# Hybrid encoder trunk on one core: the opening stage without low parts on GpSimd, and its weight pieces stored by GpSimd's queue

## The chip, the core and the metric

The program runs on one core of a Trainium2 chip. The core has a matrix engine (TensorE, PE in the rows, with its weight loads as PEld), VectorE (DVE), ScalarE (ACT), GpSimd (POOL) and SyncE (SP), which here only issues transfers. ScalarE and GpSimd issue transfers too. Each engine takes its instructions in the order in which they stand in its queue, and waits at an instruction until what it needs is there. Sixteen DMA engines move data between the memory of the chip (HBM) and the core's own memory (SBUF). The metric is the device time in microseconds of one execution; lower is better.

## The reference

Two independent batches of 512 rows by 1024 columns, `x_prompt` and `x_sample`, pass through the same layer. Only the opening of the layer matters here:

```python
c_act = jax.nn.silu(c)
mod = c_act @ w_ada[l] + b_ada[l]                      # 1024 -> 6 * 1024
sh1, sc1, g1, sh2, sc2, g2 = [m[:, None, :] for m in jnp.split(mod, N_MOD, axis=-1)]
h = rms_norm(x, norm1_g[l]) * (1.0 + sc1) + sh1
proj = h @ w_in[l]                                     # 1024 -> 2816
q_a, k_a, v_a, q_r, k_r, v_r, g_r = jnp.split(proj, IN_OFFSETS, axis=-1)
```

After it come windowed attention (on the first 768 columns of `proj`: 512 of q, 128 of k, 128 of v), bidirectional retention (the other columns), an output projection, a second modulated norm, and a squared-ReLU MLP. Weights and activations are 32-bit floats.

## The kernel before, in words

Every large product is made of three matmuls. An operand is split into a high part (a copy in the type fp32r) and a low part (the operand minus its high part); high times high, high times low and low times high are added up in a bank of PSUM. The function `mm3` (lines 128 to 130) issues the three. So every weight tile and every activation tile needs one copy (on ScalarE or VectorE) and one subtraction before the matrix engine can take it.

**The opening stage** (lines 974 to 1181) computes, for batch 0, eight column groups of 128 features, called `kc` = 0 to 7. For each group it needs the shift and scale of that group, which are sums over the whole of `w_ada` columns (`ada_sums`, matmuls of line 216 into `pm`, copied out as `mr` by ScalarE at line 221, transposed into `pmt` at line 229, added up into `mod_s` and `mod_a` by VectorE). Then `prepare` makes the modulated group `hm` from the transposed rows `xT`, and its high and low parts in `h` (lines 326 to 328). Then `products` multiplies `h` with six pieces of the matching 128 rows of `w_in` (the first 768 columns) into six open banks named `first`: 18 matmuls for a group. The rows of `x` are first normalised (`x_rstd`, `x_scale`) and transposed (`x_columns`, into banks `px`).

The weights of the stage come in three kinds. `raw_ada` of groups 0 and 1 ("ones"): four tiles of 512 KB, each by two transfers (line 985). `raw_ada` of group pairs 2, 4 and 6 ("pairs"): four tiles of 512 KB for a pair, two for the scale and two for the shift (line 89). `raw_wi`: eight tiles of 128 by 768, 384 KB each (line 89). High parts are `wh_ada` and `wih`, low parts `wl_ada` and `wil`. Before the change, the low part of every second `pairs` tile and of seven of the eight `raw_wi` tiles is computed by GpSimd, the others by VectorE; the high part of seven `raw_wi` tiles is a VectorE copy (line 1024).

The order of the work on each engine is the order in which the stage's code is written: `pin(start)` ties each instruction to the one before it on its engine, up to the products of group 5. Outside it a scheduler orders the instructions. Transfers of SP go out in order too. The tiles of the stage named by `r4` share 32 buffers, and the raw tiles of `w_in` from group 2 on share three (tag `raw`): a load waits until the last reader of the buffer's old content is done.

Batch 1 uses the same first 768 columns later (near 210 to 250 us). Its split pieces are not made again: `products` stores `wih` and `wil` of each group to HBM (line 1048, tensor `kept_first`), and `kept_unit` (line 119) loads them back, 12 loads of 512 KB: high and low parts for k, v and four pieces of q. Before the change `kept_first` is laid out so that each of the 12 loads reads 4 KB in one run per partition, and the stores, issued by ScalarE's queue, write runs of 512 bytes.

The small vectors `dec` (decays) and `sink` are loaded by GpSimd's queue, spread over 128 partitions, before the opening stage starts.

## Time and profile before

| what | value |
|---|---|
| median of 3 runs | 1155.02 us (1154.34 to 1156.5) |
| profiled execution, its own time | 1155.35 us |
| span of the profiled execution | 1153.5 us |
| TensorE busy | 1108.4 us, 96% of the span |
| VectorE busy | 899.6 us, 78% |
| ScalarE busy | 497.6 us, 43% |
| GpSimd busy | 68.2 us, 6% |

Times in rows are counted from the start of the span. In rows of the timeline the first number is the start, the second the duration, and the brackets at the end hold the idle time of that engine just before, with what ended it. In rows of groups, `x6: 1212/1221/3393` are count and shortest, median and longest duration in ns. A matmul's duration contains the pipeline's length: matmuls of 128x512 that follow each other start 0.23 us apart, whatever their duration says.

### The profile page before, as it was taken

Reading aid. Unit: us, or ns where it says so; the run is one execution under the profiler, and the core shown is the slowest. Engines: PE = TensorE matmul, PEld = TensorE weight load, DVE = VectorE, ACT = ScalarE, POOL = GpSimd, SP = SyncE. Lnnn points to the kernel's source line nnn. Section 1 sums busy time; section 2 is a strip of 40 time slices with the busy share of each in tenths; the row PEclk is TensorE's granted clock in tenths of the full one; section 3 lists DMA queues with packets and bytes.
Section 4 is the critical chain, followed back from the end, with each engine's and each line's share of the span. In section 5 each row is a group of like instructions: output and inputs, shape, how many; then the busy total and the mean of one; then the engine's idle time right before and its main releaser. Section 6 shows DMA issues by size and latency. Waiting matters only on the chain.

```text
span 1153.5 us, 14407 instructions
## 1 busy us (share of the span) xinstructions
PE 1108.4 (96%) x5167; PEld 903.5 (78%) x5167; DVE 899.6 (78%) x1496; ACT 497.6 (43%) x847; POOL 68.2 (6%) x79
## 2 busy tenths in 40 slices
PE   5989999999999999998999999999989999999995
PEld 3668787778888878887888888888778888888884
DVE  4888988978888687699998778876659655679675
ACT  4446765435554243355333333333434542335341
POOL 3620001100000000000000000000000000000011
PEclk9999999999999999999999999999999999999999
DMA  9786677665454689950655455442793455625503
GB/s 287 243 268 223 206 233 265 221 204 172 160 178 159 194 282 325 351 185 26 210 195 179 161 169 177 170 162 103 258 356 99 147 190 183 226 84 183 183 19 145
DMA packets 125135, 224.36 MB, mean 194 GB/s; under 512 B 8500, under 2 KB 59780, under 8 KB 125064
## 3 DMA queue, kind: packets, MB, share of 16 engines
q1 hardware_dynamic: 112168, 217.14, 55.9%
q10 hardware_dynamic: 12544, 6.29, 1.9%
q8 instruction: 40, 0.66, 0.2%
q0 software_dynamic: 352, 0.03, 0.2%
q14 instruction: 31, 0.25, 0.1%
HBM read 152.36 MB, written 71.06 MB: 194 GB/s over the span
## 4 chain that ended last, share of the span: by engine, by line
PE 78%; DVE 9%; DMA 7%; ACT 2%; issue 2%; POOL 1%; POOLq 0%; SPq 0%; ACTq 0%; DVEq 0%
PE x L1326 13%; PE px_None L937 12%; PE y L1326 11%; PE py_None L937 9%; PE po L129 2%; PE po L130 2%; PE po L128 2%; PE po L429 1%; PE ppt L422 1%; PE psc L396 1%; PE pj_rv L128 1%; PE pj_rv L130 1%; PE pj_rv L129 1%; PE pj_rg L130 1%; PE pj_rg L128 1%
## 5 line engine op out<-in xcount | busy, mean ns | idle before, releaser
L843 DVE TENSOR_TENSOR uc_l<-ur,uc_h 128x1024 fp32r<-128x1024 f32 x56 | 68.3, 1221 | 48.2 <-ACT uc_h L842 31.2
L1326 PE MATMUL x<-wc_h,uc_h 128*128 128x512 f32 x256 | 99.9, 391 | 4.4 <-DVE acc L1367 3.7
L1326 PE MATMUL x<-wc_l,uc_h 128*128 128x512 f32 x256 | 99.7, 390 | 0.0
L1326 PE MATMUL x<-wc_h,uc_l 128*128 128x512 f32 x256 | 99.7, 389 | 0.0
L842 ACT CAST uc_h<-ur 128x1024 fp32r<-128x1024 f32 x56 | 58.8, 1050 | 74.4 <-PE x L1326 22.7
L1326 PE MATMUL y<-wc_l,uc_h 128*128 128x512 f32 x192 | 75.6, 394 | 3.5 <-DVE wc_l L843 3.5
L1326 PE MATMUL y<-wc_h,uc_l 128*128 128x512 f32 x192 | 75.3, 392 | 0.0
L1326 PE MATMUL y<-wc_h,uc_h 128*128 128x512 f32 x192 | 75.2, 392 | 0.0
L842 ACT CAST wc_h<-w 128x1024 fp32r<-128x1024 f32 x48 | 50.4, 1050 | 49.9 <-PE x L1326 19.4
L843 DVE TENSOR_TENSOR wc_l<-w,wc_h 128x1024 fp32r<-128x1024 f32 x48 | 58.5, 1219 | 6.5 <-ACT wc_h L842 4.5
L1326 PEld LDWEIGHTS x<-wc_h,uc_h 128*128 128x128 f32 x256 | 48.1, 188 | 15.6 <-DVE acc L1367 4.5
L1326 PEld LDWEIGHTS x<-wc_h,uc_l 128*128 128x128 f32 x256 | 48.1, 188 | 10.0
L1326 PEld LDWEIGHTS x<-wc_l,uc_h 128*128 128x128 f32 x256 | 48.1, 188 | 9.9
L128 PE MATMUL po<-wh_wo,ms 128*128 128x512 f32 x128 | 50.5, 397 | 1.9 <-ACT ms L761 1.9
L129 PE MATMUL po<-wl_wo,ms 128*128 128x512 f32 x128 | 49.8, 391 | 0.3 <-DVE wl_wo L103 0.3
L130 PE MATMUL po<-wh_wo,ms 128*128 128x512 f32 x128 | 49.7, 391 | 0.0
L255 DVE SCALAR_TENSOR_TENSOR adacc_c<-raw_ada_c,cact,adacc_c 128x512 f32<-128x512 f32 x56 | 39.8, 746 | 8.6 <-DMA raw_ada_c<-in_w_ada_dram 7.6
L1326 PEld LDWEIGHTS y<-wc_l,uc_h 128*128 128x128 f32 x192 | 36.4, 190 | 11.6 <-DVE wc_l L843 4.0
L842 ACT CAST wc_s4h<-raw_w 128x1024 fp32r<-128x1024 f32 x16 | 16.9, 1054 | 62.6 <-PE px_None L937 41.6
L406 ACT ACTIVATE st<-st,negm 128x256 f32<-128x256 f32 (+1 forms) x64 | 35.2, 555 | 19.4 <-DVE negm L401 19.4
L1326 PEld LDWEIGHTS y<-wc_h,uc_l 128*128 128x128 f32 x192 | 36.5, 190 | 7.5
L1326 PEld LDWEIGHTS y<-wc_h,uc_h 128*128 128x128 f32 x192 | 36.4, 189 | 7.6
(380 smaller groups left out, 3083.3 us busy)
## 6 DMA issues: line engine op xcount, KB each, us to landing
ur<-spill SPq DMA_DIRECT2D x56, 512.0 KB, 4.1
raw_w<-in_w_mlp_dram SPq DMA_DIRECT2D x32, 512.0 KB, 3.9
spill<-s SPq DMA_DIRECT2D x64, 256.0 KB, 3.7
w<-in_w_mlp_dram SPq DMA_DIRECT2D x32, 512.0 KB, 7.0
spill<-u SPq DMA_DIRECT2D x48, 256.0 KB, 2.0
raw_ada_g<-in_w_ada_dram SPq DMA_DIRECT2D x16, 512.0 KB, 4.6
raw_ada_c<-in_w_ada_dram SPq DMA_DIRECT2D x16, 512.0 KB, 4.0
raw_ada<-in_w_ada_dram SPq DMA_DIRECT2D x12, 512.0 KB, 8.8
```

What stands on the lines that cost most here:

```text
L128: nc.tensor.matmul(ps, lhs[0], rhs[0], start=start, stop=False)
L129: nc.tensor.matmul(ps, lhs[0], rhs[1], start=False, stop=False)
L130: nc.tensor.matmul(ps, lhs[1], rhs[0], start=False, stop=stop)
L255: nc.vector.scalar_tensor_tensor(acc[b], src, cb, acc[b], ALU.mult, ALU.add)
L396: nc.tensor.matmul(psc[:, :w], qs[hh][:, isl], k_[:, s, j0 * P:j1 * P], start=(s == 0), stop=(s == 1))
L406: nc.scalar.activation(st[hh][:, :w], st[hh][:, :w], AF.Exp, bias=negm[:, hh:hh + 1], scale=0.125, accum_out=den[:, hh:hh + 1])
L422: nc.tensor.transpose(pt[:, hh * P:(hh + 1) * P], st[hh][:, jj * P:(jj + 1) * P], ident)
L429: nc.tensor.matmul(po, va[:, j0 + jj, g].rearrange("p s e -> p (s e)"), pts[jj][:, s, :], start=(jj == 0 and s == 0), stop=(jj == nj - 1 a ...
L842: nc.scalar.copy(hi, src)
L843: nc.vector.tensor_sub(lo, src, f(hi))
L937: self.last = nc.tensor.matmul(bank[:, cs], x[:, k, :], y, start=first and k == 0 and i == 0, stop=last and k == 3 and i == 2, skip_group_ ...
L1326: nc.tensor.matmul(out, left[n][x][:, i, ts_], right[n][y][:, i, :], start=first and i == 0 and k == 0, stop=end and i == 1 and k == 2, sk ...
```

## The change

What it does, in eight parts:

1. Every low part of the opening stage is computed by VectorE (`low_pair`, `low_one`, `split_wi`, `split_unit` lose their argument for the engine). Every high part `wih` is a copy on ScalarE.
2. The third and fourth row tiles of `x` no longer load one after the other: `x_2` as before, then the tiles of ones of group 0, then `x_3`, then `raw_wi` of group 0. The norm, scaling and transposing of each row tile are written out in the order of arrival, `x_3` after the sums of group 0. The conditioning vectors (`cond`) come after the transposes of `x_0` and `x_1` in the matrix engine's order.
3. The modulated group 0 is made by ScalarE alone: two activations with scale and bias, one straight into the high part, one into `hm`; VectorE only subtracts.
4. Loads of `dec` and `sink` move from before the stage to a place behind the second batch of low parts (`head_loads`); on GpSimd's queue they stand right behind the four small powers of the row norms.
5. The distance mask for the attention (`masked_distance`, three VectorE instructions on `di`) moves from the time of group 1 to just before group 2 is modulated; `sink8` moves further down.
6. `kept_first` is laid out by group of rows: the stores, now on GpSimd's queue, write runs of 3 KB, one transfer for a high or low part.
7. The 12 loads of batch 1 gather eight runs of 512 bytes for each partition.
8. The copy of `xT` of group 0 goes from ScalarE to VectorE.

```diff
-    def split_unit(src, name, lo_engine, pool=None):
+    def split_unit(src, name, pool=None):
         t = raw_unit(src, name)
         w = split_high(t, name, pool)
-        lo_engine.tensor_sub(w[1], t, f(w[0]))
+        nc.vector.tensor_sub(w[1], t, f(w[0]))
...
-            nc.sync.dma_start(f(t), kept[key][:, s, :])
             w.append(t.rearrange("p (a n) -> p a n", n=n))
+            src = kept[key][:, s]
+            nc.sync.dma_start(f(w[s]) if len(src.shape) == 3 else f(t), src)
...
+    def head_loads():
+        nc.gpsimd.dma_start(dec[:, 0, :], decay_f.broadcast_to([P, RH]))
+        nc.gpsimd.dma_start(dec[:, 1, :], decay_b.broadcast_to([P, RH]))
+        nc.gpsimd.dma_start(sink, attn_sink.broadcast_to([P, AH]))
...
+        if which == b == kc == 0:
+            for d in (dst[:, 0, :], t):
+                nc.scalar.activation(d, src, AF.Identity, bias=mod_s[0][:, kc, 0:1], scale=mod_a[0][:, kc, 0:1])
+            nc.vector.tensor_sub(dst[:, 1, :], t, f(dst[:, 0, :]))
+            return dst
...
-    xt0 += [load_x_tile(0, t) for t in range(2, NT)]
+    xt0.append(load_x_tile(0, 2))
...
-    def low_pair(kc, s, kh, engine):
+    def low_pair(kc, s, kh):
         t, w = pairs[kc, s, kh]
-        engine.tensor_sub(w[1], t, f(w[0]))
+        nc.vector.tensor_sub(w[1], t, f(w[0]))
...
-    def split_wi(kc, engine=nc.vector, low=nc.gpsimd):
+    def split_wi(kc):
         w = [r4(f"wi{s}_{kc}").rearrange("p a n -> p (a n)")[:, :768] for s in "hl"]
-        if engine is nc.scalar:
-            nc.scalar.copy(w[0], wi[kc][:, :768])
-        else:
-            nc.vector.tensor_copy(w[0], wi[kc][:, :768])
-        low.tensor_sub(w[1], wi[kc][:, :768], f(w[0]))
+        nc.scalar.copy(w[0], wi[kc][:, :768])
+        nc.vector.tensor_sub(w[1], wi[kc][:, :768], f(w[0]))
...
-                    nc.scalar.dma_start(kept_first[:, :, s, k * P:(k + 1) * P],
-                                        f(wi[k][s]).rearrange("p (c n) -> p c n", n=P))
+                    nc.gpsimd.dma_start(kept_first[:, k, s, :], f(wi[k][s]))
-    kept_first = tc.dram_tile((P, 6, 2, 1024), F32, name="kept_first")
+    kept_first = tc.dram_tile((P, KC, 2, 768), F32, name="kept_first")
     for c in range(6):
-        kept[f"in{c * P}"] = kept_first[:, c]
+        kept[f"in{c * P}"] = kept_first.rearrange("p k s n -> p s k n")[:, :, :, c * P:(c + 1) * P]
...
         ones.append(load_one(kc))
+        if kc == 0:
+            xt0.append(load_x_tile(0, 3))
         load_wi(kc)
...
-    tables = bias_tables(masked_distance())
     split_wi(1)
     high_pair(2, 1)
-    low_pair(2, 1, 0, nc.vector)
-    low_pair(2, 1, 1, nc.gpsimd)
+    low_pair(2, 1, 0)
...
     prepare(1)
+    low_pair(2, 1, 1)
     high_pair(2, 0)
-    low_pair(2, 0, 0, nc.vector)
-    low_pair(2, 0, 1, nc.gpsimd)
+    low_pair(2, 0, 0)
+    low_pair(2, 0, 1)
+    head_loads()
...
     next(g)
+    tables = bias_tables(masked_distance())
     next(tables)
     prepare(2)
```

Line numbers of the changed kernel are some 3 to 8 higher than before; names in the rows below are those of the code with a running number behind them.

The first place is GpSimd's queue in the opening stage, from the last two powers of the row norms on. Before:

```order
L306 TENSOR_TENSOR rr_x_2_198<-rv_x_2_196,neghalf 128x1
L306 TENSOR_TENSOR rr_x_3_208<-rv_x_3_206,neghalf 128x1
L1025 TENSOR_TENSOR wil_241<-raw_wi_130,wih_240 128x768
L1025 TENSOR_TENSOR wil_287<-raw_wi_138,wih_286 128x768
L1002 TENSOR_TENSOR wl_ada_2_1_1_294<-raw_ada_2_1_1_142,wh_ada_2_1_1_293 128x1024
L1002 TENSOR_TENSOR wl_ada_2_0_1_341<-raw_ada_2_0_1_146,wh_ada_2_0_1_340 128x1024
L1025 TENSOR_TENSOR wil_358<-raw_wi_148,wih_357 128x768
```

and with the change:

```order
L309 TENSOR_TENSOR rr_x_2_198<-rv_x_2_196,neghalf 128x1
L309 TENSOR_TENSOR rr_x_3_229<-rv_x_3_227,neghalf 128x1
L159 DMA dec<-in_ret_decay_fwd_dram 128x4
L160 DMA dec<-in_ret_decay_bwd_dram 128x4
L161 DMA sink<-in_attn_sink_dram 128x8
L1053 DMA kept_first<-wih_248 128x768
L1053 DMA kept_first<-wil_249 128x768
L1053 DMA kept_first<-wih_278 128x768
L1053 DMA kept_first<-wil_279 128x768
```

Thirteen subtractions are gone, and nothing but transfers is left; a store stands behind nothing but the stores before it, so it goes out as soon as its piece is split, where before it stood in ScalarE's queue behind the products of the next group.

The second place is VectorE's queue between the modulated groups 1 (`hm_0_1`) and 2 (`hm_0_2`). Before:

```order
L326 TENSOR_SCALAR hm_0_1_333<-xT_245,mod_a_103,mod_s_105 128x512
L328 TENSOR_TENSOR h_0_1_332<-hm_0_1_333,h_0_1_332 128x512
L1002 TENSOR_TENSOR wl_ada_2_0_0_338<-raw_ada_2_0_0_144,wh_ada_2_0_0_337 128x1024
L1024 CAST wih_357<-raw_wi_148 128x768
L232 COPY m_2_1_398<-pmt_1_395 128x8
L234 TENSOR_TENSOR ms_1_400<-m_2_1_398 128x4
L202 TENSOR_SCALAR mod_a_103<-ms_1_400,onep,cols 128x2 x2
L232 COPY m_2_0_435<-pmt_0_432 128x8
```

and with the change:

```order
L334 TENSOR_SCALAR hm_0_1_324<-xT_252,mod_a_100,mod_s_102 128x512
L336 TENSOR_TENSOR h_0_1_323<-hm_0_1_324,h_0_1_323 128x512
L1010 TENSOR_TENSOR wl_ada_2_1_1_286<-raw_ada_2_1_1_139,wh_ada_2_1_1_285 128x1024
L1010 TENSOR_TENSOR wl_ada_2_0_0_330<-raw_ada_2_0_0_141,wh_ada_2_0_0_329 128x1024
L1010 TENSOR_TENSOR wl_ada_2_0_1_333<-raw_ada_2_0_1_143,wh_ada_2_0_1_332 128x1024
L1030 TENSOR_TENSOR wil_353<-raw_wi_145,wih_352 128x768
L235 COPY m_2_1_393<-pmt_1_390 128x8
L237 TENSOR_TENSOR ms_1_395<-m_2_1_393 128x4
```

Three subtractions of tiles of `w_ada` and one of `w_in` stand where one subtraction and one copy stood; the three instructions on `di` follow later, between `mod_s` of this pair and `hm_0_2`.

The third place is SP's queue where batch 1 loads the kept pieces (`wh` high, `wl` low). Before:

```order
L119 DMA wl_k_2375<-kept_first 128x1024
L119 DMA wh_k_2373<-kept_first 128x1024
L119 DMA wh_v_2377<-kept_first 128x1024
L119 DMA wl_v_2379<-kept_first 128x1024
L563 DMA kept_t_115<-dtab_2_2284 128x896
```

and with the change:

```order
L121 DMA wl_k_2375<-kept_first 128x8x128
L121 DMA wh_k_2373<-kept_first 128x8x128
L121 DMA wh_v_2377<-kept_first 128x8x128
L121 DMA wl_v_2379<-kept_first 128x8x128
L121 DMA wh_q_0_2457<-kept_first 128x8x128
```

Each load is in the same place but made of eight short runs for each partition; `kept_t`, a store, has moved two loads down.

## The prediction

> **What bounds the kernel now.** I read the page first, then the opening stage by stretches of 10 us, then VectorE and GpSimd side by side in the timeline, the matrix engine's idle brackets, and the transfers of the first 90 us.

> ```profile
> span 1153.5 us, 14407 instructions
> PE 78%; DVE 9%; DMA 7%; ACT 2%; issue 2%; POOL 1%; POOLq 0%; SPq 0%; ACTq 0%; DVEq 0%
> 30.00:40.00 10.00, 7.87 (x46) 5.14 (x45) 9.24 (x8) 4.99 (x7) 7.95 (x5) 0.87 0.53 175
> 40.00:50.00 10.00, 9.66 (x51) 6.89 (x49) 8.11 (x12) 4.39 (x8) 4.07 (x3) 0.96 0.98 315
> 60.00:70.00 10.00, 7.82 (x51) 5.14 (x49) 8.36 (x17) 4.27 (x8) 4.40 (x3) 1.00 0.86 243
> ```

> The chain that ends last is 78% matrix engine, so time can only be won where that engine idles. The change touches the opening stage, and there it does. The rows of stretches give the busy time of PE, PEld, DVE, ACT and POOL, the granted clock, and the DMA share with GB/s: between 30 and 40 us the matrix engine works 7.87 us, VectorE is busy 9.24 us with only eight instructions, and the clock falls to 0.87. Why eight instructions fill 9 us, the timeline shows:

> ```profile
> 27.39 1.22 DVE L1002 TENSOR_TENSOR wl_ada<-raw_ada,wh_ada 128x1024 fp32r<-128x1024 f32 x1
> 29.45 1.16 DVE L326 TENSOR_SCALAR hm<-xT,mod_a,mod_s 128x512 f32<-128x512 f32 x1
> 33.34 3.39 DVE L1002 TENSOR_TENSOR wl_ada<-raw_ada,wh_ada 128x1024 fp32r<-128x1024 f32 x1
> 37.51 4.01 DVE L202 TENSOR_SCALAR mod_a<-ms,onep,cols 128x2 f32<-128x2 f32 x2
> ...
> 70.52 1.29 DVE L234 TENSOR_TENSOR ms<-m 128x4 f32<-128x4 f32 x1
> ...
> 33.24 2.41 POOL L1002 TENSOR_TENSOR wl_ada<-raw_ada,wh_ada 128x1024 fp32r<-128x1024 f32 x1 [0.37 <-ACT wh_ada L97]
> 37.33 1.83 POOL L1025 TENSOR_TENSOR wil<-raw_wi,wih 128x768 fp32r<-128x768 f32 x1 [1.68 <-issue]
> 39.12 2.37 POOL L1002 TENSOR_TENSOR wl_ada<-raw_ada,wh_ada 128x1024 fp32r<-128x1024 f32 x1
> ```

> The same subtraction takes VectorE 1.22 us alone and 3.39 us when GpSimd works from 33.24 to 35.65; two tiny instructions that start at 37.51 end at 41.5, when GpSimd's second piece ends. From 29.45 to 70.52 eleven instructions are stretched so; against their ordinary lengths the excess is 16.9 us. [...]

> What reaches the matrix engine is less than 16.9 us. These are the places that I use as checkpoints (the second matmul of a group waits for the low part of `h`):

> ```profile
> 24.94 0.50 PE L129 MATMUL first<-h,wih 128*128 128x512 f32 x1 [0.22 <-DVE h L328]
> 36.79 0.28 PE L216 MATMUL pm<-wl_ada,c 128*4 128x256 f32 x1 [1.77 <-DVE wl_ada L1002]
> 40.87 0.28 PE L229 MATMUL pmt<-ident,mr 4*128 4x4 f32 x2
> 44.17 0.39 PE L129 MATMUL first<-h,wih 128*128 128x512 f32 x1
> 58.62 0.50 PE L129 MATMUL first<-h,wih 128*128 128x512 f32 x1 [0.85 <-DVE h L328]
> 66.08 0.28 PE L229 MATMUL pmt<-ident,mr 4*128 4x4 f32 x2 [2.10 <-ACT mr L221]
> 74.09 0.50 PE L129 MATMUL first<-h,wih 128*128 128x512 f32 x1
> 82.54 0.39 PE L130 MATMUL first<-h,wil 128*128 128x512 f32 x1
> ```

> Groups 0, 2, 4 and 6 start (by their second matmul) at 24.94, 44.17, 58.62 and 74.09, and the last product starts at 82.54. Behind that the matrix engine is nearly full, so I let a gain at the end of the stage go through to the end of the program.

> **The change part by part.** Durations for the moved pieces, from the groups of the two raw tiles:

> ```profile
> L1025 POOL TENSOR_TENSOR wil<-raw_wi,wih x7: 1827/1854/2767, 18.2 to 69.9; 128x768 fp32r<-128x768 f32 x7
> L1024 DVE CAST wih<-raw_wi x7: 547/552/554, 26.9 to 74.2; 128x768 fp32r<-128x768 f32 x7
> L1022 ACT CAST wih<-raw_wi x1: 832/832/832, 17.3 to 17.3; 128x768 fp32r<-128x768 f32 x1
> L1025 DVE TENSOR_TENSOR wil<-raw_wi,wih x1: 959/959/959, 74.8 to 74.8; 128x768 fp32r<-128x768 f32 x1
> L97 ACT CAST wh_ada<-raw_ada x14: 1038/1044/1053, 14.6 to 64.7; 128x1024 fp32r<-128x1024 f32 x14
> L1002 POOL TENSOR_TENSOR wl_ada<-raw_ada,wh_ada x6: 2371/2482/2587, 30.3 to 65.8; 128x1024 fp32r<-128x1024 f32 x6
> ```

> VectorE gains six subtractions of 1.22 and seven of 0.96 us, 14.0 us; it loses seven copies of 0.55 (3.9 us) and the 16.9 us of stretching: 6.8 us less over the stage. ScalarE gains seven copies of 0.83, 5.8 us, and loses the issuing of 16 stores. But the subtractions now stand in one queue where two engines worked side by side, so the totals settle nothing; I walk the chain between checkpoints.

> *To group 0.* Before, the square sum of `x_2` waits for its transfer:

> ```profile
> 11.69 1.06 ACT L317 ACTIVATE jk<-x 128x1024 bf16<-128x1024 f32 x1 [1.54 <-DMA x<-in_x_prompt_dram]
> 15.09 2.82 PE L1068 MATMUL px<-ident,x 128*128 128x128 f32 x12 [2.27 <-DVE x L321]
> GB/s 38 351 94 232 365 277 287 313 340 350 347 374 370 348 357 185 4 22 330 317 352 307 289 267 126 157 0 177 167 351 346 344 162 380 357 371 231 369 401 362
> q0 software_dynamic: 96, 0.01, 2.1%
> raw_ada<-in_w_ada_dram SPq DMA_DIRECT2D x12, 512.0 KB, 8.8
> raw_wi<-in_w_in_dram SPq DMA_DIRECT2D x8, 384.0 KB, 5.8
> kept_first<-wih ACTq DMA_DIRECT2D x8, 384.0 KB, 4.6
> ```

> The GB/s row has 40 slices of 2.25 us. In the third and fourth (4.5 to 9 us) the rate is 94 and 232 against some 350 later: 2.3 us of transfer lost, while the 96 small packets of `dec` and `sink` on GpSimd's queue take 2.1% of 90 us, 1.9 us of all sixteen engines. Moved away, I let all early loads land 2.3 us sooner. Then ScalarE's order holds: `x_1` is scaled by 8.6, its transposes and the conditioning transpose end by 10.3, and the square sum of `x_2` starts at 10.9. From there in sequence: square 1.25, power 0.7, scale 0.75, six transposes 1.4 (half of the 2.82 row), sixteen sums 2.65, `mr` 0.4, `wih` 0.85, `wil` 0.95, `xT` 0.65, `mod` 0.4, two activations 1.2, subtraction 0.7: 22.8 us, against 24.94. Gain 2.1; if the transfers came no sooner, 1.3.

> *To group 2.* Here the stores decide. They now go out as soon as a piece is split, from about 19 us on, and loads run at the full 350 GB/s until 35 us (slice 16). A store of 384 KB costs 1.1 us of that, and `wih` and `wil` of groups 0 and 1 and perhaps `wih` of 2 come in this time: 4.4 to 5.5 us; `dec` and `sink` return here with 1.9. ScalarE must split both scale tiles of pair 4 before it copies out the second `mr` of pair 2, in both versions. By bytes, the second tile lands before at 32.4 us (10 MB up to 35 us, 1.4 MB of them behind it, and some 1.5 us more for the slowest engine). After: 32.4 - 2.3 + 1.9 + 4.4 to 5.5 = 36.4 to 37.5, then the copy 1.05, `mr` 0.36 and a step: `pmt` starts at 37.9 to 39.0, against 40.87. Without the stores VectorE's row of four subtractions would give 36. From `pmt` to group 2: sums and `mod` 0.95, `di` 1.3 (new in this place), `hm` 0.5, ScalarE 0.65, subtraction 0.7: 4.15 us against 3.3 before, and products of group 1 cover only 2.9 of it. Group 2 starts at 42.05 to 43.15, I take 42.6: gain 1.6 us.

> *To groups 4, 6 and the end.* After group 2 VectorE subtracts twice (2.35), `wil` 0.9, `hm` 0.5, ScalarE `h` 0.65 and two copies 1.95, `mr` 0.35: `pmt` 6.65 behind the checkpoint; three matmuls, sixteen sums, three matmuls and a transpose 3.7; sums, `mod` and `hm` 1.35; two copies of the next pair and the bias table 1.4 beyond, `h` 0.65, its subtraction 0.7: 14.0 to 14.05, against 14.45 before (58.62 - 44.17). Group 4 to 6 in the same way gives 14.65 against 15.47, and the last 36 matmuls run at 0.228 without the stop before group 7: 8.2 against 8.67, with 0.4 for ScalarE's queue free of stores. Together 2.0 us. Gain at the end of the stage: 1.6 + 2.0 = 3.6 us.

> *Batch 1.* The gather makes 1024 runs of 512 bytes of a load that was 128 runs of 4 KB. Such a form stands in the trace: `raw_rq`, also 1024 runs of 512 bytes.

> ```profile
> L89 SPq DMA_DIRECT2D raw_rq<-in_w_in_dram x4: 385/441/783, 96.1 to 166.6; - x4
> DMA to landing us min/median/max: 4.9/4.9/4.9
> wh_q<-kept_first SPq DMA_DIRECT2D x4, 512.0 KB, 4.9
> 246.53 0.50 PE L130 MATMUL pj_q<-h,wl_q 128*128 128x512 f32 x1 [0.79 <-DMA wl_q<-kept_first]
> ```

> Issue 0.44 us and 4.9 us to land, like the present `wh_q`: below, nothing. Above: the first transfers of `w_ada`, in 512-byte runs, moved 277 to 313 GB/s (slices 6 to 8) against 350 to 400, up to 0.6 us more for each load; at 246.53 a `wl_q` is late already, and three late loads would be 1.8. I take 0.8.

> Sum: 3.6 - 0.8 = 2.8 us. The profiled execution took 1155.35 us, so 1152.5 of its kind; it lies 0.3 above the median of 1155.02, so I forecast **1152.2 us**. A measurement of this kernel can tell 0.2% (2.3 us) from no change.

> **Rivals.** (a) *The stores do not bind.* If GpSimd's queue sends them slowly or between the loads, `pmt` comes at 36 and group 2 at about 40: 2.5 us more, 1149.7. For it: the DMA engines idle from 35 to 40 us. Against: 1.09 of their time was taken from 20 to 30.

> (b) *Transfers take it all.* If the packets of 3 KB win more than their share against the 512 and 1024-byte runs of `w_ada`, the pieces of pair 2 are late too, the matrix engine idles over 2 us near 25 and loses clock, as it did after the 1.77 us stop (0.87 and 0.96 in two stretches of 10 us are 1.7 us). That costs 1.7 again and `pmt` comes at 40 or later: the stage keeps 1 us, the gather takes it: 1155.0.

> (c) *Slower, by the gather.* Twelve loads with 0.6 us more are 7.2 us of transfer between 207 and 250. If `wl_q` and `wh_q` are on the path at each of six column units, half of that counts: 3.6, with a gain of only 2: 1156.6. It decides if the DMA share there nears 1; one stop of 0.79 us speaks against six.

> (d) *GpSimd still stops VectorE.* Sixteen stores need some 0.6 us each of GpSimd's own time (by the row below). If these stop VectorE like its subtractions did, a third of the 9.6 us on the path costs 3.2: 1155.4. Against it, the one neighbourhood in the trace:

> ```profile
> 209.94 0.57 POOL L292 DMA_DIRECT2D gates<-adacc_g  x1 [6.88 <-ACT adacc_g L291]
> 210.02 0.68 DVE L494 SCALAR_TENSOR_TENSOR mix<-pyb,rg 128x512 f32<-128x512 f32 x1
> ```

> VectorE keeps its 0.68 us beside it. [...]

> **How the numbers follow.** Forecast 0.42, (a) 0.17, (b) 0.24, (c) 0.10, (d) 0.07. The forecast's own range is 1150.6 to 1153.8 (`pmt` 37.4 to 40, gather 0 to 1.8). The range that leaves out no more than 2 in 10 reaches into (a) and past (b): 1148.8 to 1156.0. Two thirds of the forecast and all of (a) lie over 2.3 us below 1155.02, with a little of the others 0.50; (c) and a remainder are slower, 0.12; the rest, 0.38, can't be told.

> **What would show it.** VectorE's subtractions at 1.22 throughout and no instruction of 3 or 4 us; square of `x_2` near 10.9, group 0 at 22.8; a ScalarE wait for `raw_ada` of pair 4 that ends at 36 to 38; group 2 at 42.6, the last product near 79. The forecast fails if the matrix engine waits over 2 us for pair 2 near 26 us, if `wl_q` waits add more than 2 us, or if the time won at 80 us is gone by 150.

## The result, and the profile after

| | before | changed |
|---|---|---|
| median of nine runs each | 1154.89 us (1152.05 to 1158.74) | 1149.65 us (1146.01 to 1152.17) |
| ratio, with its 95% interval | 1 | 0.995 (0.9936 to 0.9964) |
| profiled execution, own time | 1155.35 us | 1149.65 us |
| its span | 1153.5 us | 1147.9 us |
| first matmul of `pj_rv`, behind the stage | 82.76 us | 77.34 us |
| from the 700th to the 1150th matmul | 99.28 us | 96.00 us |
| from the 1150th to the last matmul | 887.67 us | 890.36 us |

The change won 0.5%, 4.2 to 7.4 us. The forecast was 1152.2 with a range from 1148.8 to 1156.0. The last three rows of the table are taken from the matrix engine's list of matmuls, which has 5167 in each trace (numbered from 0). They say that the profiled execution had won 5.4 us by the end of the stage and 8.6 by the 1150th matmul (near 250 us), and lost 2.7 of that again in the long rest, mostly at half clock (taken up under what stays open).

The page of the changed kernel, its span and the chain that ended last:

```profile
span 1147.9 us, 14427 instructions
PE 78%; DVE 8%; DMA 7%; ACT 3%; issue 2%; SPq 1%; POOL 1%; POOLq 0%; ACTq 0%; DVEq 0%
```

The three stretches that the prediction showed, with the same columns (PE, PEld, DVE, ACT, POOL, granted clock, DMA share, GB/s):

```profile
30.00:40.00 10.00, 9.20 (x56) 6.09 (x55) 7.77 (x17) 5.65 (x9) 1.08 (x2) 1.00 1.06 390
40.00:50.00 10.00, 8.34 (x50) 5.87 (x50) 8.65 (x13) 4.96 (x8) 1.62 (x3) 1.00 0.92 324
60.00:70.00 10.00, 8.49 (x47) 6.33 (x46) 8.65 (x24) 6.34 (x11) 1.62 (x3) 1.00 0.79 272
```

Between 30 and 40 us VectorE now does 17 instructions in 7.77 us where it did 8 in 9.24, the matrix engine works 9.20 us in place of 7.87, and its clock is 1.00 in place of 0.87. The timeline shows the subtractions at their own length (three in 3.49 us, two in 2.35), and one store on GpSimd's queue:

```profile
30.16 3.49 DVE L1010 TENSOR_TENSOR wl_ada<-raw_ada,wh_ada 128x1024 fp32r<-128x1024 f32 x3
40.94 2.35 DVE L1010 TENSOR_TENSOR wl_ada<-raw_ada,wh_ada 128x1024 fp32r<-128x1024 f32 x2
...
20.31 0.54 POOL L1053 DMA_DIRECT2D kept_first<-wil  x1 [0.45 <-DVE wil L1030]
```

The prediction's checkpoints on the matrix engine, in the same timeline:

```profile
23.27 0.50 PE L130 MATMUL first<-h,wih 128*128 128x512 f32 x1 [0.93 <-DVE h L332]
36.67 0.28 PE L232 MATMUL pmt<-ident,mr 4*128 4x4 f32 x2 [0.69 <-ACT mr L224]
41.08 0.50 PE L130 MATMUL first<-h,wih 128*128 128x512 f32 x1 [0.23 <-DVE h L336]
55.10 0.39 PE L130 MATMUL first<-h,wih 128*128 128x512 f32 x1
69.41 0.39 PE L130 MATMUL first<-h,wih 128*128 128x512 f32 x1
77.34 0.39 PE L129 MATMUL pj_rv<-wh_rv,h 128*128 128x512 f32 x1
```

| checkpoint | before | forecast | measured |
|---|---|---|---|
| group 0 | 24.94 | 22.8 | 23.27 |
| second `pmt` of pair 2 | 40.87 | 37.9 to 39.0 | 36.67 |
| group 2 | 44.17 | 42.6 | 41.08 |
| group 4 | 58.62 | | 55.10 |
| group 6 | 74.09 | | 69.41 |
| first `pj_rv` | 82.76 | near 79 | 77.34 |

So the stage gained 5.4 us where 3.6 were forecast, nearly all of the difference before group 2. And the 0.8 us that the gather should have cost do not appear; that stretch is faster.

### The profile page after: what moved, and what is told of

It is laid out like the page before. It is cut to its first block, busy times and chain, and to the rows that moved or that the text cites. A ratio compares the mean times of both kernels' runs of the same rounds, so it can differ in the third digit from the quotient of the medians.

```text
span 1147.9 us, 14427 instructions
## 1 busy us (share of the span) xinstructions
PE 1106.3 (96%) x5167; PEld 903.1 (79%) x5167; DVE 893.1 (78%) x1502; ACT 501.9 (44%) x854; POOL 46.6 (4%) x82
## 4 chain that ended last, share of the span: by engine, by line
PE 78%; DVE 8%; DMA 7%; ACT 3%; issue 2%; SPq 1%; POOL 1%; POOLq 0%; ACTq 0%; DVEq 0%
PE x L1329 13%; PE px_None L945 13%; PE y L1329 12%; PE py_None L945 9%; PE po L130 2%; PE po L131 2%; PE po L129 2%; DMA w<-in_w_mlp_dram 1%; PE ppt L430 1%; PE po L437 1%; PE psc L404 1%; DMA raw_ada<-in_w_ada_dram 1%; PE pj_rv L129 1%; PE pj_rv L131 1%; PE pj_rv L130 1%
## 5 line engine op out<-in xcount | busy, mean ns | idle before, releaser
L1329 PEld LDWEIGHTS x<-wc_h,uc_h 128*128 128x128 f32 x256 | 48.4, 189 | 15.7 <-DVE acc L1370 4.5
L1329 PEld LDWEIGHTS x<-wc_l,uc_h 128*128 128x128 f32 x256 | 48.4, 189 | 10.0
L129 PE MATMUL po<-wh_wo,ms 128*128 128x512 f32 x128 | 50.5, 397 | 1.7 <-ACT ms L769 1.7
L130 PE MATMUL po<-wl_wo,ms 128*128 128x512 f32 x128 | 49.8, 391 | 0.7 <-DVE wl_wo L103 0.7
L1329 PEld LDWEIGHTS y<-wc_l,uc_h 128*128 128x128 f32 x192 | 36.7, 191 | 12.5 <-DVE wc_l L851 4.8
L258 DVE SCALAR_TENSOR_TENSOR adacc_c<-raw_ada_c,cact,adacc_c 128x512 f32<-128x512 f32 x56 | 39.8, 745 | 6.9 <-DMA raw_ada_c<-in_w_ada_dram 5.8
L414 ACT ACTIVATE st<-st,negm 128x256 f32<-128x256 f32 (+1 forms) x64 | 35.3, 556 | 18.4 <-DVE negm L409 18.4
L1329 PEld LDWEIGHTS y<-wc_h,uc_h 128*128 128x128 f32 x192 | 36.6, 191 | 7.8
L1329 PEld LDWEIGHTS y<-wc_h,uc_l 128*128 128x128 f32 x192 | 36.6, 191 | 7.6
## 6 DMA issues: line engine op xcount, KB each, us to landing
ur<-spill SPq DMA_DIRECT2D x56, 512.0 KB, 4.7
raw_w<-in_w_mlp_dram SPq DMA_DIRECT2D x32, 512.0 KB, 3.8
w<-in_w_mlp_dram SPq DMA_DIRECT2D x32, 512.0 KB, 7.5
raw_ada_g<-in_w_ada_dram SPq DMA_DIRECT2D x16, 512.0 KB, 4.2
raw_ada_c<-in_w_ada_dram SPq DMA_DIRECT2D x16, 512.0 KB, 4.3
raw_ada<-in_w_ada_dram SPq DMA_DIRECT2D x12, 512.0 KB, 10.0
```

The costliest lines, as they stand in the source:

```text
L129: nc.tensor.matmul(ps, lhs[0], rhs[0], start=start, stop=False)
L130: nc.tensor.matmul(ps, lhs[0], rhs[1], start=False, stop=False)
L258: nc.vector.scalar_tensor_tensor(acc[b], src, cb, acc[b], ALU.mult, ALU.add)
L414: nc.scalar.activation(st[hh][:, :w], st[hh][:, :w], AF.Exp, bias=negm[:, hh:hh + 1], scale=0.125, accum_out=den[:, hh:hh + 1])
L1329: nc.tensor.matmul(out, left[n][x][:, i, ts_], right[n][y][:, i, :], start=first and i == 0 and k == 0, stop=end and i == 1 and k == 2, sk ...
```

## The experiments

Twelve runs. For each: the time of the first `pj_rv` in its profile (the stage), the stretch from the 700th to the 1150th matmul, the rest up to the last matmul, and the ratio of its times to those of the kernel before measured beside it, with the 95% interval.

| kernel | first `pj_rv` | 700 to 1150 | 1150 to last | ratio |
|---|---|---|---|---|
| before | 82.76 | 99.28 | 887.67 | 1 |
| before, a second profile (e11) | 82.49 | 97.55 | 889.72 | |
| changed | 77.34 | 96.00 | 890.36 | 0.9950 (0.9936 to 0.9964) |
| changed, low parts back on GpSimd (e1) | 83.73 | 96.06 | 892.46 | 1.0012 (0.9998 to 1.0026) |
| changed, stores and layout as before (e2) | 81.47 | 97.95 | 892.66 | 0.9999 (0.9980 to 1.0018) |
| changed, stores by ScalarE's queue (e3) | 77.25 | 98.90 | 891.22 | 0.9967 (0.9952 to 0.9983) |
| changed, old layout (e4) | 79.04 | 95.95 | 891.21 | 0.9957 (0.9943 to 0.9972) |
| before, part 1 alone (e5) | 80.04 | 97.84 | 889.29 | 1.0007 (0.9995 to 1.0019) |
| before, parts 6 and 7 alone (e6) | 83.50 | 96.32 | 888.88 | 1.0003 (0.9993 to 1.0013) |
| changed, `dec` and `sink` first (e7) | 77.41 | 96.06 | 891.48 | 0.9968 (0.9957 to 0.9978) |
| changed, first stores held (e8) | 77.40 | 96.23 | 887.21 | 0.9951 (0.9935 to 0.9967) |
| changed, two moves (e9) | 75.68 | 96.44 | 890.15 | 0.9965 (0.9953 to 0.9978) |
| changed, all moves (e10) | 76.58 | 96.53 | 888.76 | 0.9957 (0.9940 to 0.9975) |
| before, parts 1, 6 and 7 (e12) | 77.82 | 96.24 | 888.56 | 0.9978 (0.9965 to 0.9992) |

### The low parts back on GpSimd

```diff
-        nc.vector.tensor_sub(w[1], t, f(w[0]))
+        (nc.gpsimd if kh else nc.vector).tensor_sub(w[1], t, f(w[0]))
...
-        nc.vector.tensor_sub(w[1], wi[kc][:, :768], f(w[0]))
+        (nc.vector if kc == 7 else nc.gpsimd).tensor_sub(w[1], wi[kc][:, :768], f(w[0]))
```

> The changed kernel with one part undone: GpSimd again computes the low part of every second pair tile and of seven of the eight pieces of w_in, as before. Head, transfers, stores, layout and the order on the matrix engine and on SP's queue stay as changed. Theory (the stage was won by ending VectorE's stops): subtractions of 3 to 4 us return on VectorE between 29 and 71 us; group 0 keeps its start near 23.3, the second pmt of pair 2 falls from 36.7 back to 39 or later, and the first matmul of pj_rv from 77.3 to 80.5 to 82; about 3 to 4.5 us lost, nothing lost behind the stage, so some 1153.5 in place of 1149.65. Rival (the earlier head and the stores' new queue carry the stage): pj_rv within 1 us of 77.3, time within 1 us of the changed kernel.

Measured: the first `pj_rv` at 83.73, 6.4 us later than in the changed kernel and later than before the change. The head was even faster (group 0 at 22.29, since VectorE had less to do there); all of the loss lies behind 36 us. VectorE, GpSimd and the matrix engine in the timeline of this run:

```profile
33.74 6.00 DVE L205 TENSOR_SCALAR mod_a<-ms,onep,cols 128x2 f32<-128x2 f32 x2
...
35.50 1.88 POOL L1030 TENSOR_TENSOR wil<-raw_wi,wih 128x768 fp32r<-128x768 f32 x1
37.30 2.40 POOL L1010 TENSOR_TENSOR wl_ada<-raw_ada,wh_ada 128x1024 fp32r<-128x1024 f32 x1
...
43.00 0.79 PE L129 MATMUL first<-h,wih 128*128 128x512 f32 x1 [4.44 <-ACT h L335]
...
44.75 0.63 PE L129 MATMUL first<-h,wih 128*128 128x512 f32 x1
45.17 0.63 PE L130 MATMUL first<-h,wih 128*128 128x512 f32 x1
```

Two tiny VectorE instructions last until 39.74, when GpSimd's second subtraction ends; the modulation of group 2 is late by that, and the matrix engine stops for 4.44 us. Then its matmuls start 0.43 us apart where 0.23 is the usual distance: they run at half clock until 48.4, which is some 2.7 of the 6.4 us. The theory stands in its cause. Its price was under-rated by 2 to 3 us, and the place was another: the second `pmt` of pair 2 came at 35.34, not at 39 or later, and VectorE's stop stands behind it. The two instructions that took 6.00 us here took 0.50 in the changed kernel. The first 1.8 us of the 6.00 lie beside GpSimd's issuing of `dec` and `sink` (33.62 to 35.50), which stand behind its subtractions in this run; why VectorE stood still there too is not shown.

### The stores: queue and layout apart

The stores and the 12 loads as before, that is, the changes on `kept_first` and the one in `kept_unit` undone (only the store's lines are shown, here and in the third diff):

```diff
-                    nc.gpsimd.dma_start(kept_first[:, k, s, :], f(wi[k][s]))
+                    nc.scalar.dma_start(kept_first[:, :, s, k * P:(k + 1) * P],
+                                        f(wi[k][s]).rearrange("p (c n) -> p c n", n=P))
```

> The changed kernel with parts 6 and 7 undone: the stores of wih and wil go back to ScalarE's queue in runs of 512 bytes, the 12 loads of batch 1 read 4 KB in one run again. The program order that follows the stage then is that of the kernel before: with the stores in ScalarE's queue the scheduler places 428 of the later matmuls differently. Theory (the 2.2 us won between the 1000th and the 1150th matmul come from that order, which hangs on the queue of the stores, and not from the layout): stage within 1 us of the changed kernel's (first pj_rv at 77 to 78.5), 1000th to 1150th matmul 35 us again as before (changed: 32.9), time 1151.5 to 1153. Rival (the stores' form decides the stage, as the old runs of 512 bytes are slower for the DMA engines): pj_rv at 79 or later.

Only the queue:

```diff
-                    nc.gpsimd.dma_start(kept_first[:, k, s, :], f(wi[k][s]))
+                    nc.scalar.dma_start(kept_first[:, k, s, :], f(wi[k][s]))
```

> The changed kernel with only the queue of the stores undone: ScalarE issues them, in runs of 3 KB, and batch 1 gathers as in the changed kernel. The later matmuls stand in the order of before. Theory (order, not layout): like the run with both parts undone, 1000th to 1150th matmul 35 us, and not more, since a gather costs nothing that the matrix engine sees; time 1151.5 to 1153. By my prediction's term for the gather (0.8, bounds 0 to 1.8) it would be 0.8 slower than that run. Rival (the gather itself, or its landing time, won the 2.2 us): 33 us, time as the changed kernel's.

Only the layout:

```diff
-                    nc.gpsimd.dma_start(kept_first[:, k, s, :], f(wi[k][s]))
+                    nc.gpsimd.dma_start(kept_first[:, :, s, k * P:(k + 1) * P],
+                                        f(wi[k][s]).rearrange("p (c n) -> p c n", n=P))
```

> The changed kernel with only the layout undone: GpSimd's queue issues the stores, but in the old layout (runs of 512 bytes), and the loads of batch 1 read 4 KB in one run. The matrix engine's order is that of the changed kernel throughout. Theory (order, not layout): first pj_rv within 0.7 us of 77.3, 1000th to 1150th matmul 32.5 to 33.3, time within 1 us of the changed kernel. My prediction's term: 0.8 faster behind the stage. Rival (the gather won the time): 35 us, time 1152. [...]

Measured, in the stage: `pj_rv` at 81.47 with both undone, 77.25 with the queue alone undone, 79.04 with the layout alone undone. My theory that the stage would not move was wrong; the rival on the stores' form holds, with two different mechanisms.

On ScalarE's queue the form decided by ScalarE's own time. ScalarE near 45 us, first with runs of 512 bytes (e2):

```profile
44.44 0.67 ACTq L1052 DMA_DIRECT2D kept_first<-wil  x1
45.15 1.05 ACT L97 CAST wh_ada<-raw_ada 128x1024 fp32r<-128x1024 f32 x1 [0.70 <-issue]
47.05 0.36 ACT L223 COPY mr<-pm 4x256 f32<-4x256 f32 x1
```

and with rows of 3 KB (e3):

```profile
44.58 0.45 ACTq L1053 DMA_DIRECT2D kept_first<-wil  x1
45.06 1.05 ACT L97 CAST wh_ada<-raw_ada 128x1024 fp32r<-128x1024 f32 x1 [0.25 <-issue]
46.96 0.36 ACT L224 COPY mr<-pm 4x256 f32<-4x256 f32 x1
```

The copies wait 0.70 us for the stores' issue against 0.25. So `mr` stands later behind the matrix engine's last work, and the engine's stop before `pmt` grows from 1.43 to 1.87 us (`pmt` itself moves by only 0.09). The granted clock, in the column after POOL, shows what this half microsecond costs. First e2, then e3:

```profile
47.00:48.00 1.00, 0.54 (x3) 0.49 (x4) 1.00 (x2) 1.00 (x4) 0.00 (x0) 0.97 1.03 284
49.00:50.00 1.00, 1.00 (x7) 0.56 (x6) 1.00 (x3) 0.00 (x0) 0.00 (x0) 0.50 1.02 136
50.00:51.00 1.00, 1.00 (x6) 0.60 (x5) 0.24 (x1) 0.00 (x0) 0.00 (x0) 0.50 0.86 334
```

```profile
47.00:48.00 1.00, 0.63 (x4) 0.57 (x5) 1.00 (x2) 1.00 (x4) 0.00 (x0) 1.00 1.05 372
49.00:50.00 1.00, 1.00 (x12) 0.74 (x9) 1.00 (x3) 0.00 (x0) 0.00 (x0) 1.00 0.97 369
50.00:51.00 1.00, 1.00 (x7) 0.57 (x4) 0.16 (x1) 0.52 (x2) 0.00 (x0) 1.00 0.59 231
```

Seven matmuls in a microsecond against twelve, for some 3.4 us; the next `pmt` comes at 52.67 against 51.01. The same happens behind a stop of 2.51 us at 64.36, and so 4.2 us are lost in all.

On GpSimd's queue the form decided by the transfers. A store took 0.79 us to issue in place of 0.54, which nothing waited for, but ScalarE's copies of pair 4's scale tiles waited longer for their loads (e4; in the changed kernel these two rows read 33.88 with 1.02 and 35.30 with 0.38):

```profile
35.60 1.05 ACT L97 CAST wh_ada<-raw_ada 128x1024 fp32r<-128x1024 f32 x1 [2.24 <-DMA raw_ada<-in_w_ada_dram]
37.00 1.04 ACT L97 CAST wh_ada<-raw_ada 128x1024 fp32r<-128x1024 f32 x1 [0.35 <-DMA raw_ada<-in_w_ada_dram]
```

This is 1.7 us later, as much as the difference at the end of the stage (79.04 against 77.34). It is one execution of each; two executions with the same stores can lie 1 us apart in this place (e9 below).

Behind the stage: with the stores on ScalarE's queue the stretch takes 97.95 and 98.90, on GpSimd's 95.95 and 96.00, and the layout makes little difference in either pair (0.05 us with the new order; 0.95 with the old, of which one stop for `wl_q` in e3 is 0.54). The likely cause is the order: the scheduler places several hundred of the matmuls between the 332nd and the 1166th otherwise, depending only on which queue issues the stores (by the traces, e2 and e3 have the order of before there, e4 that of the changed kernel). No run changes the order alone. Over all traces the five with the old order took 97.55 to 99.28 and the nine with the changed kernel's or nearly its order 95.95 to 96.53. The gather cost nothing that can be told from these traces; the kernel before, which gathers nothing, has a stop for `wl_q` too, in one of its two profiles.

### Parts done alone

Part 1 alone, on the kernel before:

```diff
-        engine.tensor_sub(w[1], t, f(w[0]))
+        nc.vector.tensor_sub(w[1], t, f(w[0]))
...
-            nc.vector.tensor_copy(w[0], wi[kc][:, :768])
-        low.tensor_sub(w[1], wi[kc][:, :768], f(w[0]))
+        nc.scalar.copy(w[0], wi[kc][:, :768])
+        nc.vector.tensor_sub(w[1], wi[kc][:, :768], f(w[0]))
```

> The kernel before with part 1 alone: every low part of the stage on VectorE, every wih on ScalarE; head, stores on ScalarE's queue in runs of 512 bytes, contiguous loads and the later order as before. GpSimd's share alone cost the changed kernel 6.4 us of the stage when it was put back. Theory (three conditions must hold together: no GpSimd subtraction, stores in long rows, and a matrix engine whose stops stay under some 1.8 us; if one fails, ScalarE's mr comes late and the clock falls to half behind the stop): VectorE without stretched instructions, but ScalarE held behind its stores as in the run with parts 6 and 7 undone; first pj_rv at 81 to 82.5, time within 1.5 us of before. Rival (the low parts alone carry the gain): pj_rv at 77.5 to 79, time 1150 to 1151.5.

Parts 6 and 7 alone, on the kernel before (the lines for the layout and the loads, as in the change, are left out):

```diff
-                    nc.scalar.dma_start(kept_first[:, :, s, k * P:(k + 1) * P],
-                                        f(wi[k][s]).rearrange("p (c n) -> p c n", n=P))
+                    nc.gpsimd.dma_start(kept_first[:, k, s, :], f(wi[k][s]))
```

> The kernel before with parts 6 and 7 alone: stores on GpSimd's queue in rows of 3 KB, gathered loads; GpSimd also keeps its subtractions, head and VectorE's work as before. The later matmuls stand in the changed kernel's order. Theory (the stage belongs to VectorE's stops, the part behind the stage to the order): first pj_rv at 81.5 to 84, the 700th to the 1150th matmul take 96.0 us as in the changed kernel (99.3 before), time 1151.5 to 1154. Rival (the stores' form frees the stage by itself, 4.2 us as between the two runs with stores on ScalarE): pj_rv at 78.5 to 79.5, time 1150.

Both of these together (the diffs of the two, on the kernel before):

> The kernel before with parts 1, 6 and 7 and nothing else: low parts on VectorE, stores on GpSimd's queue in rows of 3 KB, gathered loads; the head (dec and sink first, x_3 behind x_2, group 0's modulation, the conditioning's place, di at group 1) as before. Part 1 alone and parts 6 and 7 alone each left the time where it was. Theory (these two are what the gain needs, each opens the way for the other, and the head's 1.7 us at group 0 are swallowed by the landing of pair 4): group 0 at 24.5 to 25, pmt of pair 2 at 36.5 to 38, first pj_rv at 77.3 to 78.5, the 700th to the 1150th matmul 96 us, time 1149.5 to 1151.5, ratio to before 0.995 to 0.9975. Rival (the head is needed too: without it group 0's 1.7 us stay lost, or a stop costs the clock): pj_rv at 79 to 80.5, ratio 0.998 to 1.000.

Measured: neither part alone moves the time (1.0007 and 1.0003). Part 1 alone had won 2.6 us of the stage in its profile, less than the rival's 4 and more than my theory allowed. With it ScalarE stands behind its stores exactly as in e2, and the stop of 1.68 us was followed by the half clock:

```profile
45.83 1.05 ACT L97 CAST wh_ada<-raw_ada 128x1024 fp32r<-128x1024 f32 x1 [0.70 <-issue]
...
48.14 0.28 PE L229 MATMUL pmt<-ident,mr 4*128 4x4 f32 x2 [1.68 <-ACT mr L221]
```

Parts 6 and 7 alone leave VectorE's stops and the stage as they were (83.50). Together they give 77.82, 4.8 us of the stage's 5.3, where the two single gains in the stage add up to 1.7 (2.6 and -0.9; all against 82.6, the mean of the two profiles of before). Each opens the way for the other. As I read it, without GpSimd's subtractions the stage is short enough for ScalarE's half microseconds to count, and without the stores on ScalarE's queue VectorE's gain reaches the matrix engine. The measured time gained 0.22% (0.08 to 0.35), just under the range that I had expected and less than the stage and the stretch would make it; this is taken up below.

### The head

```diff
+    head_loads()
...
     low_pair(2, 0, 1)
-    head_loads()
```

> The changed kernel with part 4 undone: dec and sink are loaded before the stage again. My prediction took 2.3 us off the landing of every early load for this part and let it go through to group 0 (0.8 of it against its lower bound). Theory now (the matrix engine's place at the second scale tile of pair 4 is set by bytes, and dec and sink only trade places with other bytes): square sum of x_2 at 11.5 to 12 in place of 10.8, group 0 at 24 to 24.8 in place of 23.3, but pmt of pair 2 within 0.6 of 36.7 and pj_rv within 0.6 of 77.3; time within 1 us of the changed kernel. By the prediction's sum: 1 to 1.5 us slower all the way.

Measured: `dec` and `sink` do delay `x_2`. Its load is issued at 3.4 us in both kernels and lands 3.8 us behind that in the changed kernel, 7.3 us with `dec` and `sink` first:

```profile
L147 SPq DMA_DIRECT2D x<-in_x_prompt_dram x1: 424/424/424, 3.4 to 3.4; - x1
DMA to landing us min/median/max: 3.8/3.8/3.8
```

```profile
L147 SPq DMA_DIRECT2D x<-in_x_prompt_dram x1: 415/415/415, 3.4 to 3.4; - x1
DMA to landing us min/median/max: 7.3/7.3/7.3
```

But the square sum of `x_2` starts at 10.71, as in the changed kernel (10.78), since in both it stands behind the tanh on ScalarE:

```profile
10.59 0.22 ACT L178 ACTIVATE cth<-cols 128x16 f32<-128x16 f32 x1 [3.93 <-DVE cols L176]
10.71 1.04 ACT L322 ACTIVATE jk<-x 128x1024 bf16<-128x1024 f32 x1
```

It landed at 10.7, just in time; in e12, where `x_3` loads right behind it as before the change, it took 8.2 us. What reaches group 0 are 0.56 us (23.83): ScalarE waits 0.58 and 0.60 us for the two tiles of ones of group 0, for which it does not wait in the changed kernel. `pmt` of pair 2 came 0.08 later (36.75), `pj_rv` 0.07. Where `dec` and `sink` are loaded has no effect at the end of the stage.

### The stores held back

```diff
+    gate = small([P, 1], "gate")
+    nc.gpsimd.tensor_scalar(gate, f(pairs[4, 1, 1][0][:, 0, 0, 0:1]), 1.0, None, ALU.mult)
     products(1, 2, 6)
```

> The changed kernel, with a one-element instruction on GpSimd that reads the second scale tile's high part of pair 4, put ahead of the first store: the stores of groups 0 to 2 cannot start before that tile has landed and been copied. This measures the prediction's store term (4.4 to 5.5 us of delay for that tile). Theory (the early stores take little, since they share the time rather than add all their bytes ahead of the tile; with ScalarE's late stores pmt stood at 36.2): pmt at 35.3 to 36.3, group 2 at 39.8 to 40.8, first pj_rv 76.3 to 77.3, time 0 to 1 us below the changed kernel. By the prediction's term: pmt at 31 to 32.5 by bytes, held at 34 to 36 by VectorE's row; or, if the held stores crowd the loads of pair 6, pj_rv over 78.

Measured: the landing of the first scale tile of pair 4 stands in the groups of the raw tiles, taken for 19.5 to 22 us, where its transfer is issued (the first number behind the durations) and landed (the last row). In the changed kernel and in this one:

```profile
L89 SPq DMA_DIRECT2D raw_ada<-in_w_ada_dram x2: 378/1720/3062, 19.7 to 20.2; - x2
DMA to landing us min/median/max: 14.1/14.1/14.1
```

```profile
L89 SPq DMA_DIRECT2D raw_ada<-in_w_ada_dram x2: 1248/1356/1463, 20.6 to 21.9; - x2
DMA to landing us min/median/max: 10.1/10.1/10.1
```

It lands at 33.8 with the early stores and at 30.7 without: they delay it by 3.1 us (by the same rows of e4, 20.1 and 15.4, the old layout delays it by 4.8). In e3, whose first store goes out at 44.2, it lands at 29.5 (19.8 and 9.7), which makes the delay 4.3; so these traces give 3.1 to 4.3 us. But ScalarE, in this run:

```profile
33.45 2.00 ACT L97 CAST wh_ada<-raw_ada 128x1024 fp32r<-128x1024 f32 x2
36.06 0.36 ACT L224 COPY mr<-pm 4x256 f32<-4x256 f32 x1 [0.61 <-PE pm L219]
```

It copies both tiles without waiting for a transfer, and yet the second `mr` starts at 36.06 (36.26 in the changed kernel), now 0.61 us behind the matrix engine's `pm`, that is behind VectorE's row. Two limits lie 0.2 us apart here, and taking one away gains nothing: `pmt` at 36.59, `pj_rv` at 77.40, both just above what I had expected.

### Two attempts to win more

Two pieces of work moved into idle times of their engines (the diff leaves out the same hoist inside the loop):

```diff
     split_wi(3)
+    high_pair(4, 0)
     prepare(3)
...
     next(g)
+    tables = bias_tables(masked_distance())
     products(1, 1, 2)
     next(g)
-    tables = bias_tables(masked_distance())
     next(tables)
```

> The changed kernel with two pieces of work put where their engine is idle. The three di instructions on VectorE (1.3 us) go ahead of the second pmt of pair 2, into the 2.06 us in which VectorE waits for that pmt (35.3 to 37.4); the two copies of the shift tiles of the pairs 4 and 6 on ScalarE (2.0 us) go ahead of h of groups 3 and 5, into ScalarE's waits of 3.6 and 2.9 us for hm, so that mr of the scale does not stand behind them. Theory (what is left of the stage are the matrix engine's stops of 0.69 at group 2, 1.07 and 1.51 at the pmt of pairs 4 and 6): group 2 at 40.4, pmt of pair 4 at 46.0 to 46.8 (47.5), of pair 6 at 59.7 to 60.7 (61.8), first pj_rv at 75.3 to 76.2 in place of 77.3; 1.2 to 2 us off the time. Rival (the low parts on VectorE come late next, so the stops only move to pm): pj_rv within 0.5 of 77.3.

and besides these the square sum of `x_2` ahead of the tanh, `hm` of group 0 on VectorE, and the gate of the last run:

```diff
-    for _ in range(3):
-        next(cond)
-    x_scale(xt0[2], x_rstd(0, 2, xt0[2]))
+    r2 = x_rstd(0, 2, xt0[2])
+    next(cond)
+    x_scale(xt0[2], r2)
     x_columns(2)
+    for _ in range(2):
+        next(cond)
```

> The kernel of the last run, and besides: the square sum of x_2 ahead of the conditioning's tanh on ScalarE (x_2 lands at 7.2, its square sum began at 10.8), hm of group 0 on VectorE beside ScalarE's h, and the gate that holds the first stores until pair 4's second scale tile is copied. Each alone was seen to be, or should be, swallowed by the next limit (without the gate the tile's landing at 35.3, with the gate the row of VectorE's subtractions that ends at 36.1). Theory (two limits stand within 1 us of each other at that place, so only both moves together gain): pmt of pair 2 at 34.3 to 35.5, group 0 at 20.8 to 21.8, group 2 at 38.2 to 39.5, first pj_rv at 73.3 to 74.8, time 2.5 to 4 us below the changed kernel. Rival (the held stores or pair 6's loads take it back between 45 and 60): group 2 as said, but pj_rv at 75 or later.

Measured: the two moves took the stops at the `pmt` of pairs 4 and 6 away (46.08 and 58.81, against 47.49 and 61.81) and the stage was 1.66 us shorter, as expected, although pair 4's first scale tile was copied a microsecond later in this execution than in the changed kernel's (33.88):

```profile
34.84 1.05 ACT L97 CAST wh_ada<-raw_ada 128x1024 fp32r<-128x1024 f32 x1 [2.20 <-DMA raw_ada<-in_w_ada_dram]
...
46.08 0.28 PE L232 MATMUL pmt<-ident,mr 4*128 4x4 f32 x2
58.81 0.28 PE L232 MATMUL pmt<-ident,mr 4*128 4x4 f32 x2
```

With all moves group 0 came at 21.73, but then ScalarE waited 1.43 us for pair 2's second scale tile and the matrix engine stopped before `pmt`; it is the shortest stop in any of these traces that was followed by half clock. The stage ended at 76.58, not at 73.3 to 74.8:

```profile
24.40 1.04 ACT L97 CAST wh_ada<-raw_ada 128x1024 fp32r<-128x1024 f32 x1 [1.43 <-DMA raw_ada<-in_w_ada_dram]
...
25.76 0.28 PE L232 MATMUL pmt<-ident,mr 2*128 2x2 f32 x2 [1.55 <-ACT mr L224]
...
27.00:28.00 1.00, 1.00 (x5) 0.92 (x4) 0.17 (x1) 0.56 (x1) 0.00 (x0) 0.50 1.05 390
```

Neither version's time can be told from the changed kernel's: 0.9965 and 0.9957, with intervals that overlap its 0.9936 to 0.9964. No version that beats it was found.

### The kernel before, once more

> The kernel before once more, for a second profile: how much of a difference between two profiles belongs to the kernel and how much to the execution. If the half clock at 37.4 to 40.8 and the wl_q stops near 245 and 253 belong to the kernel, the first pj_rv stands at 82.0 to 83.5 again and the 700th to the 1150th matmul take 98.8 to 99.8. If they belong to the execution, pj_rv can stand at 80.5 to 81.5 and the stretch at 97.5 to 98.5.

Measured: `pj_rv` at 82.49 and the half clock behind 36.6 again, so the stage belongs to the kernel. The stretch took 97.55: of its 99.28 in the first profile 1.7 us belonged to the execution, 1.07 at the stop for `wl_q` at 246.53 and 0.67 at one for VectorE's `ryn` at 253.57. The order is thus worth 1.5 to 3 us, not 3.3.

## Why the prediction was right, and where it was not

The sign, the place and half of the cause held. The stage cannot win while GpSimd's subtractions stop VectorE: putting them back costs 6.4 us. But ending the stops was not enough. With the old stores on ScalarE's queue the changed kernel loses 4.1 us of the stage and all of the measured gain (0.9999), and part 1 alone gains nothing measured; the prediction had the stores as a cost, and only 0.4 us of gain for taking them off ScalarE's queue. The measured 1149.65 is within the range from 1148.8 to 1156.0 but outside the forecast's own, 1150.6 to 1153.8: 2.5 us off the forecast and on the number of rival (a). That (a) fits so well is in part luck, since neither sum has the order of the later matmuls in it. Step by step:

- **The start of group 0: 22.8 forecast, 23.27 measured.** The two activations took 0.81 and 0.80 us where I had put 1.2 for both. The reading of `dec` and `sink` held: `x_2` lands 3.5 us sooner without them ahead of it (I had put 2.3), and then ScalarE's order holds its square sum, 10.78 where I had put 10.9. At group 0 they are worth 0.56 us where the sum had 0.8, at the end 0.07. The other parts at the head (`x_3`'s place, the activations, the copy of `xT`) were not run alone, so their shares are not shown.
- **The start of group 2: the mis-sized term.** "4.4 to 5.5 us" of stores ahead of pair 4's second scale tile, and 1.9 of `dec` and `sink`, put `pmt` at 37.9 to 39.0. The second tile landed at 35.3 where I had put 36.4 to 37.5, and `pmt` came at 36.67. The stores measured 3.1 us at that pair's first tile in one pair of executions and 4.3 in another, so part of the miss is the stores' price and part may be the base of 32.4 us that I had worked out by bytes. Moving `dec` and `sink`, which I had put at 2.3 us less and 1.9 more here, came to 0.08. Why the stores cost less than their bytes is not shown. My own aside, that VectorE's row would give 36 without the stores, was confirmed at 36.59. With the runs of 512 bytes `pmt` came 1.7 later (38.36), within my forecast: I had priced both forms alike.
- **From group 2 to the end: 2.0 forecast, 2.3 measured** (5.42 less 3.09). One leg was right by luck: from group 2 to group 4 the terms that I listed add up to 14.45, which is no gain, not to the 14.0 that I wrote and that was measured (14.02).
- **The gather: 0.8 forecast, nothing measured** (96.00 against 95.95 in the pair that differs by the layout).
- **Not in the sum at all: the order of the later matmuls.** I had read the program's order only for the stage. With the new order the stretch from 153 to 249 us is 1.5 to 3 us shorter.
- **Rivals.** (a) gave 1149.7, by the right place and partly the right reason: the stores do delay the tile, but hardly bind. (b) is refuted by the stop before pair 2's `pmt`, 0.52 us near 26; (c) by the pair with and without the gather; (d) by VectorE's rows in the changed kernel, where the twelve subtractions of the pairs' tiles took 1.217 to 1.226 us beside sixteen stores (the one row that did not keep its length, beside the issuing of `dec` and `sink`, is in the first experiment).

**What stays open.** The gain by the 1150th matmul is larger than the measured gain for every kernel here. The changed kernel should have won 7.7 us by the first two columns of the table (against the mean of the two profiles of before, 82.6 and 98.4) and won 5.8; e12 should have won 7.0 and won 2.5. Part of it is the base: both profiled executions of before (1155.35 and 1155.29) stand 0.4 to 1.9 us above its medians beside the other kernels (1153.39 to 1154.89). The rest of the program, with the same instructions, took 887 to 893 us in these profiles, and the two profiles of before alone differ by 2.0. In the profiles this is accounted for. The matrix engine's stops in the rest add up to 14.5 to 17.1 us, and it worked 3 to 11 us of it at half clock; with the stops and half of that time taken off, the rest is 869.7 to 870.5 us in all fourteen. So the 2.7 us that the changed kernel's profile lost there are 2.4 us of half clock and 0.4 of longer stops, not work. The half clock came mostly near 850 and 1120 us, where the matrix engine stops for 3 to 5 and for 2.9 us, and it lasted for a time that differs from execution to execution (10.2 us of these two places in the changed kernel's profile, 3.4 in that of before). In the changed kernel's profile and in that of before:

```profile
851.00:854.50 3.50, 3.50 (x11) 2.75 (x10) 3.50 (x4) 0.31 (x1) 0.00 (x0) 0.60 0.62 185
1120.50:1124.00 3.50, 3.37 (x9) 2.70 (x10) 1.59 (x4) 0.73 (x2) 1.67 (x4) 0.57 0.32 120
```

```profile
859.00:862.50 3.50, 3.50 (x15) 2.77 (x14) 3.50 (x5) 0.41 (x1) 0.00 (x0) 0.86 0.62 200
1128.50:1132.00 3.50, 3.50 (x17) 2.87 (x16) 1.67 (x3) 0.72 (x2) 2.01 (x4) 1.00 0.09 33
```

The runs of one kernel follow it roughly: the changed kernel's fastest, 1146.01, had a mean granted clock of 0.999, and its slowest, 1152.17, had 0.992 (as had the profiled one, 1149.65); e12's range from 1148.29 at 0.997 to 1153.42 at 0.992. Whether a kernel's early part changes how often these late windows come, or the ratios of e5, e9 and e12 merely scatter, these runs do not tell.

## What to carry to other kernels

When two engines' work is put in one queue, look for what comes next within a microsecond: here VectorE's stops, the stores' form and ScalarE's issue lay so close that two changes, each worth nothing measurable alone (1.0007 and 1.0003), together gave nearly all of the stage's gain (4.8 of 5.3 us), and some of the time's. Price a store by what the engine that issues it and the loads beside it lose, and by its form, not by its bytes alone (here the same bytes in another form moved the end of the stage by 4.2 us on ScalarE's queue and by 1.7 on GpSimd's). And read the order of the whole program, not only of the stage that was edited: which queue issues a transfer can move hundreds of instructions behind it.

## What the runs showed of the hardware that was not expected

**A store's form changed its issue time on both queues:** 384 KB took 0.33 us on ScalarE's queue in 3 KB rows (e3) and 0.52 in runs of 512 bytes (before) at the least, up to 1.25 and 2.24 where several followed each other; on GpSimd's 0.54 (the changed kernel) and 0.79 (e4).
